# Threading a weight-streaming matmul stage through a VectorE-bound stage, matmul by matmul

## The chip, the cores and the metric

The kernel runs on one core of a Trainium2 chip. The metric is the device time of one execution in microseconds (us). The kernel before has a median of 1814.12 us over three runs (1813.09 to 1814.47). One more execution was profiled; all rows of "the profile" and "the trace" are from it. The engines are TensorE (PE; its weight loads are listed as PEld), VectorE (DVE), ScalarE (ACT), GpSimd (POOL) and SyncE (SP), which here only issues DMAs.

## The reference

One decoder layer over 512 tokens of width 1024 in float32. A convolution branch and a sliding-window attention branch are gated and added to the residual. Then comes a product-key expert layer (PEER): per token and head, two score vectors over 128 keys; the best 16 of each give the best 16 of their sums; so each token has 8 x 16 = 128 experts out of 128 x 128 = 16384, with softmax gates. Cut to what matters:

```python
def chunk(args):                                   # 128 tokens
    hx, idx, g = args                              # idx, g: 128 experts and gates per token
    a = jax.nn.gelu(jnp.einsum("ced,cd->ce", u_emb[idx], hx), approximate=False)
    return jnp.einsum("ce,ced->cd", g * a, v_emb[idx])
```

The tables u_emb and v_emb have 16384 rows of 1024 floats (4 KB each). The output is the residual plus this sum, normalised by its root mean square.

## The kernel before

**The expert layer in two ways.** Tokens 0 to 127 (`ROW_CHUNKS`) are done by gathering: for each of the 128 slots an indirect DMA on GpSimd's queue (`gathered`, L634) fetches 128 rows, one per token and 512 KB in all; VectorE multiplies and sums it (L649 for u, L657 for v). `by_rows` is a generator: each `next` emits one gather and its VectorE instruction, 256 in all, and a 257th call emits the norm and the store of these tokens (`finish`). The other 384 tokens (`DENSE`, three blocks) are done densely: for each of 128 blocks of 128 experts, a *U step* computes gelu(U x) for all 384 tokens (24 matmuls of 384 columns into a PSUM tile `mm`, then ScalarE's L674 into `ga`), and a *V step* multiplies the result with a gate matrix that is mostly zero and with V (18 matmuls of 512 columns into six PSUM tiles that accumulate over all 128 steps).

**Weights.** Float32 products are made of three products of split operands. `load_w` fetches a 512 KB block on SP's queue (`wraw`, three buffers), ScalarE rounds it (`whi`, L131), and the rest `wlo` is made either by VectorE (L137), or, while `by_dma` is set (the heads and the gate matrix), by ScalarE negating (L134) and a GpSimd DMA that adds the block again (L135). `whi` and `wlo` have four buffers each. `products` issues 16 matmuls with `whi` and then 8 with `wlo`.

**The stages that the change touches.** (1) Eight heads: `head(h)` computes scores (two blocks of 24 matmuls of 512 columns, then score matmuls L523) and the choice of experts, mostly VectorE; behind each, `U_HEADS[h]` U steps are emitted. (2) The gate matrix: for each dense token block, `keys` transposes the chosen keys, and `build_g` makes, for four tokens at a time, two comparison matrices on VectorE (`yt` L618, `xt` L621, two buffers each), multiplies them on TensorE (L626, four matmuls of 128 columns: a *gate chunk*, PSUM tile `sc`, two buffers), and ScalarE copies the result into `gst` (L628). Every 8 chunks VectorE makes `xa` and `xb` anew (L610, L612); every 4 chunks `gst` (two buffers) is stored to DRAM, 1 MB. There are 96 chunks in 24 groups. Between groups `up` emits U steps, 11 spread evenly, and three at the end (`U_LAST`). (3) The V loop: step i emits U step i + 42 (`AHEAD`) as long as there is one (86 steps), then V step i. Gate values are loaded back for eight steps at a time (`gl`, L683, two buffers), VectorE multiplies them with `ga` (L688, eight short instructions), ScalarE and VectorE split the product (`wh` L692, `wl` L693, two buffers each), and TensorE takes it (L699 to L701).

**What sets the order.** The program is written in one order, and a scheduler reorders each engine's instructions by its own estimate of when operands are ready. So the order on TensorE is not the written one: U steps whose weights are ready move ahead of gate chunks that wait for VectorE. Once built, each engine runs its list strictly in that order. The gathers in the V loop are paced by the variable `due` (L750): a U step adds twice as much as a step without one.

Of the kernel before, what the change touches and what calls it, by code (L numbers as in the profile page):

```python
# [17 lines left out]
P = 128  # L18
D = 1024
KB = D // P  # L20
S = 512
# [8 lines left out]
SLOTS = HEADS * TOPK  # L30
# [3 lines left out]
ROW_CHUNKS = (0,)  # L34
DENSE = tuple(b for b in range(NB) if b not in ROW_CHUNKS)
BUILT = DENSE
ND = len(DENSE)
NU = ND * P
CAND = 80

AHEAD = 42
U_HEADS = (4, 4, 4, 4, 3, 3, 3, 3)
U_LAST = 3
ROWS = 4
GT = 16
GI = 8
R_G = 0.0
R_V = 0.96
UC = 3
N_TAPS = 7  # L50
XT = 4
# [28 lines left out]
def body(ctx: ExitStack, tc: tile.TileContext, a, out):  # L80
    nc = tc.nc
# [9 lines left out]
    def psum(tag):  # L91
        return ps.tile([P, S], F32, name=tag, tag=tag, bufs=2)
# [19 lines left out]
    pace = [None]  # L112
# [10 lines left out]
    def fetch(src):  # L123
        raw = wp.tile([P, D], F32, name="wraw", bufs=WRAW)
        nc.sync.dma_start(raw, src)
        return raw

    def load_w(src):
        raw = fetched.pop(0) if fetched else fetch(src)
        hi = wp.tile([P, D], F32R, name="whi", bufs=WHL)  # L130
        nc.scalar.activation(hi, raw, AF.Copy)  # L131
        lo = wp.tile([P, D], F32R, name="wlo", bufs=WHL)
        if by_dma[0]:
            nc.scalar.activation(lo, hi.bitcast(F32), AF.Copy, scale=-1.0)  # L134
            nc.gpsimd.dma_start(lo, src, accum_op=OP.add)  # L135
        else:
            nc.vector.tensor_tensor(lo, raw, hi.bitcast(F32), op=OP.subtract)  # L137
        return hi, lo

    def products(p, w, x):  # L140
        wh, wl = w
        xh, xl = x
        for k in range(KB):
            ks = slice(k * P, (k + 1) * P)
            nc.tensor.matmul(p, wh[:, ks], xh[:, k], start=(k == 0), stop=False)  # L145
            nc.tensor.matmul(p, wh[:, ks], xl[:, k], start=False, stop=False)  # L146
        for k in range(KB):
            ks = slice(k * P, (k + 1) * P)
            pace[0] = nc.tensor.matmul(p, wl[:, ks], xh[:, k], start=False, stop=(k == KB - 1))  # L149

    def mm_block(src, x):
        w = load_w(src)
        p = psum("mm")
        products(p, w, x)
        return p
# [41 lines left out]
    def pair_x(name):  # L197
        return [keep.tile([P, KB, S], F32R, name=name + x, tag="x" + x) for x in "hl"]
# [225 lines left out]
    p = psum("ot")  # L424
# [12 lines left out]
    p = psum("ot")  # L437
# [11 lines left out]
    for j in range(KB):  # L449
        p = mm_block(a["w_ao"][j], oT)  # L450
        nc.vector.tensor_tensor(sga[:, j], sga[:, j], p, op=OP.mult)
    mT = pair_y("m")
    for j in range(KB):
        p = mm_block(a["w_co"][j], yT)
# [10 lines left out]
    tT = pair_x("tT")  # L465
    by_dma[0] = False
    for b0 in range(0, NB, 2):
        acc = [psum(t) for t in (("ot", "ot", "sc", "sc") if b0 == 0 else ("sc", "sc", "mm", "mm"))]
        for k in range(KB):
            hi, lo = load_w(a["w_out"][k])  # L470
            for c in range(2):
                for n in range(2):
                    ns = slice(n * 512, (n + 1) * 512)
                    p, cs = acc[2 * c + n], chunk(b0 + c)
                    nc.tensor.matmul(p, mT[0][:, k, cs], hi[:, ns], start=(k == 0), stop=False)
                    nc.tensor.matmul(p, mT[1][:, k, cs], hi[:, ns], start=False, stop=False)
            for c in range(2):
                for n in range(2):
                    ns = slice(n * 512, (n + 1) * 512)
                    nc.tensor.matmul(acc[2 * c + n], mT[0][:, k, chunk(b0 + c)], lo[:, ns], start=False,  # L480
                                     stop=(k == KB - 1))
# [115 lines left out]
    def build_g(b):  # L597
        n = BUILT.index(b)
        p = psum("tr")
        nc.tensor.transpose(p[:, :P], gate[:, b], ident)  # L600
        gT = rt.tile([P, P], F32, name="gT", bufs=2)
        nc.scalar.activation(gT, p[:, :P], AF.Copy)
        high = P // LOW
        for g in range(P // GT):
            if g * GT % XS == 0:
                xa = gp.tile([P, XS, high], F32, name="xa")
                xb = gp.tile([P, XS, LOW], F32, name="xb")
                cs = slice(g * GT, g * GT + XS)
                for t, w, k in ((xa, high, 0), (xb, LOW, 1)):
                    nc.vector.tensor_tensor(t, keyT[:, k, n, cs, None].to_broadcast([P, XS, w]),  # L610
                                            iota[:, None, :w].to_broadcast([P, XS, w]), op=OP.is_equal)
                nc.vector.tensor_tensor(xa, xa, gT[:, cs, None].to_broadcast([P, XS, high]), op=OP.mult)  # L612
            st = gp.tile([P, P, GT], F32, name="gst", bufs=2)
            for t0 in range(0, GT, XT):
                c = slice(g * GT + t0, g * GT + t0 + XT)
                cx = slice(c.start % XS, c.start % XS + XT)
                yt = gp.tile([P, XT, P], F32, name="yt", bufs=XB)
                nc.vector.tensor_tensor(yt, keyT[:, 2, n, c, None].to_broadcast([P, XT, P]),  # L618
                                        iota[:, None, :].to_broadcast([P, XT, P]), op=OP.is_equal)
                xt = gp.tile([P, XT, high, LOW], F32, name="xt", bufs=XB)  # L620
                nc.vector.tensor_tensor(xt, xa[:, cx, :, None].to_broadcast([P, XT, high, LOW]),  # L621
                                        xb[:, cx, None, :].to_broadcast([P, XT, high, LOW]), op=OP.mult)
                for t1 in range(0, XT, 4):
                    p = psum(("sc", "ot")[t1 // 4 % 2]).rearrange("p (t i) -> p t i", t=4)
                    for t in range(4):
                        nc.tensor.matmul(p[:, t], yt[:, t1 + t], xt[:, t1 + t].rearrange("p a b -> p (a b)"),  # L626
                                         start=True, stop=True)
                    nc.scalar.activation(st[:, :, t0 + t1:t0 + t1 + 4].rearrange("p i t -> p t i"), p, AF.Copy)  # L628
            nc.sync.dma_start(gv[b][:, g], st)
            yield  # L630

    def gathered(table, b, s):
        r = rows.tile([P, D], F32, name="row", bufs=ROWS)
# [32 lines left out]
    ga = {}  # L666
    gl = {}

    def u_step(i):
        w = load_w(a["put"][i])  # L670
        p = psum("mm")[:, :NU]
        products(p, w, [t[:, :, S - NU:] for t in tT])
        g = tp.tile([P, NU], F32, name="ga", bufs=AHEAD + 1)
        nc.scalar.activation(g, p, AF.Gelu)  # L674
        ga[i] = g
# [33 lines left out]
    ups = iter(range(P))  # L709

    def up(n):
        for _ in range(n):
            i = next(ups, None)
            if i is not None:
                u_step(i)

    for h in range(HEADS):
        head(h)
        up(U_HEADS[h])
    spread, groups, done = AHEAD - U_LAST - sum(U_HEADS), len(BUILT) * (P // GT), 0  # L720
    for b in BUILT:
        keys(b)
        for _ in build_g(b):
            up((done + 1) * spread // groups - done * spread // groups)
            done += 1
    up(U_LAST)
    by_dma[0] = False
    gctx.close()
    vp = ctx.enter_context(tc.tile_pool(name="vp", bufs=1, reuse_waits="tile"))
# [1 line left out]
    gf = load_g("gf")  # L731
    vacc = [psum(t) for t in ("tr", "sc", "ot") for _ in range(2)]
    rowgen = by_rows()
    total, due = 2.0 * P - AHEAD, 0.0
    load_gates(0)
    last = {}
    for i in range(P):
        up(1)
        if 0 <= i % GI - GL_AT < ND:
            load_gates(i - i % GI + GI, (i % GI - GL_AT,))  # L740
        if i < P - 2:
            v_steps(i)
        elif i == P - 2:
            for _ in rowgen:
                pass
            for n, b in enumerate(DENSE):
                last[n] = rows.tile([P, D], F32, name="row", bufs=ROWS)
                nc.sync.dma_start(last[n], x2d[b])
            v_steps(i, i + 1)
        due += (2 if i + AHEAD < P else 1) * 2 * SLOTS * len(ROW_CHUNKS) / (R_V * total)  # L750
        while due >= 1:
            due -= 1
            next(rowgen, None)
# [59 lines left out]
```

## Time and profile before

| what | value |
|---|---|
| the profiled execution's own time | 1814.3 us |
| its span, first to last instruction | 1812.5 us |
| mean granted TensorE clock | 0.980 |
| TensorE busy | 1726.6 us, 95% |
| VectorE busy | 1362.7 us, 75% |
| ScalarE busy | 907.1 us, 50% |
| GpSimd busy | 457.4 us, 25% |
| first and last gate chunk on TensorE | 702.2 and 887.8 us |
| first V matmul | 901.67 us |
| moved by DMA | 444.86 MB, mean 245 GB/s |

Busy times are sums over the whole program. The stages have different limits, so the rows to read are those of a stretch of time. A row that ends in brackets says how long the engine stood idle before it and what ended the wait.

### The profile page before, as it was taken

What the parts mean: (1) busy time and instruction counts of PE and PEld (TensorE: products, weight loads), DVE (VectorE), ACT (ScalarE), POOL (GpSimd) and SP (SyncE); (2) the same over time, 40 slices, a digit from 0 to 9 for tenths busy, and PEclk for the clock granted to TensorE, in tenths of its full rate; (3) what the DMA queues carried; (4) which work ended last, traced back from release to release, by engine and by line L of the source; (5) the groups of instructions that cost most, each with busy time, mean ns of one, the idle gap of its engine ahead of it and who ended that gap; (6) DMA issues with size and microseconds to landing.
All of it is one profiled execution on the core that took longest, in us unless ns stands there. A gap on an engine that the chain in (4) does not pass through costs nothing.

```text
span 1812.5 us, 25036 instructions
## 1 busy us (share of the span) xinstructions
PE 1726.6 (95%) x8892; PEld 1514.8 (84%) x8892; DVE 1362.7 (75%) x2755; ACT 907.1 (50%) x1287; POOL 457.4 (25%) x374
## 2 busy tenths in 40 slices
PE   7999999999999999977599999999999999999996
PEld 6887767788899999976489999999998999987775
DVE  6999992745777996688678768768768777887775
ACT  6449988645656657666433333333333333333323
POOL 1111100110111111000034335335335434434430
PEclk9999999999999999999799999999999999999998
DMA  8996554776999989743678898898888888888873
GB/s 246 225 222 148 130 116 105 166 221 213 252 215 225 212 209 245 226 178 163 232 275 294 286 353 299 288 328 315 283 319 315 306 316 316 316 310 286 289 274 105
DMA packets 165709, 444.86 MB, mean 245 GB/s; under 512 B 14544, under 2 KB 66256, under 8 KB 162512
## 3 DMA queue, kind: packets, MB, share of 16 engines
q0 software_dynamic: 53280, 194.01, 39.9%
q1 hardware_dynamic: 112304, 249.26, 38.6%
q8 instruction: 70, 1.15, 0.2%
q14 instruction: 55, 0.45, 0.1%
HBM read 410.44 MB, written 29.88 MB: 243 GB/s over the span
## 4 chain that ended last, share of the span: by engine, by line
PE 65%; issue 15%; POOL 7%; DVE 6%; DMA 5%; ACT 2%; SPq 0%; POOLq 0%; DVEq 0%; ACTq 0%
PE mm L146 14%; PE mm L145 14%; PE mm L149 14%; POOL row L634 7%; PE sc L626 4%; DMA row<-pv,eidx 2%; PE tr L700 2%; PE tr L701 2%; PE tr L699 2%; PE sc L699 2%; PE sc L700 2%; DMA gl<-gb 2%; PE ot L699 2%; PE sc L701 2%; PE ot L700 2%
## 5 line engine op out<-in xcount | busy, mean ns | idle before, releaser
L131 ACT ACTIVATE whi<-wraw 128x1024 fp32r<-128x1024 f32 x346 | 365.3, 1057 | 447.1 <-DMA wraw<-put 172.3
L145 PE MATMUL mm<-tTh,whi 128*128 128x384 f32 (+2 forms) x1168 | 395.3, 340 | 1.5 <-ACT wlo L134 1.4
L146 PE MATMUL mm<-tTl,whi 128*128 128x384 f32 (+2 forms) x1168 | 396.5, 340 | 0.2 <-DVE tTl L192 0.2
L137 DVE TENSOR_TENSOR wlo<-wraw,whi 128x1024 fp32r<-128x1024 f32 x232 | 283.1, 1223 | 51.0 <-ACT whi L131 50.1
L634 POOL DMA_INDIRECT row<-pu,eidx x128 | 176.2, 1377 | 402.7 <-DVE row L649 254.4
L634 POOL DMA_INDIRECT row<-pv,eidx x128 | 182.2, 1424 | 255.1 <-DVE acc L657 241.2
L149 PE MATMUL mm<-tTh,wlo 128*128 128x384 f32 (+2 forms) x1168 | 234.8, 339 | 0.0
L145 PEld LDWEIGHTS mm<-tTh,whi 128*128 128x128 f32 x1168 | 219.6, 188 | 10.0 <-ACT wlo L134 1.8
L146 PEld LDWEIGHTS mm<-tTl,whi 128*128 128x128 f32 x1168 | 219.5, 188 | 8.3 <-DVE tTl L192 0.4
L149 PEld LDWEIGHTS mm<-tTh,wlo 128*128 128x128 f32 x1168 | 204.0, 188 | 3.8
L692 ACT ACTIVATE wh<-gl 128x384 fp32r<-128x384 f32 x128 | 67.1, 524 | 274.2 <-PE ot L700 255.3
L657 DVE SCALAR_TENSOR_TENSOR acc<-row,gate,acc 128x1024 f32<-128x1024 f32 x128 | 164.1, 1282 | 13.7 <-DMA row<-pv,eidx 7.3
L649 DVE SCALAR_TENSOR_TENSOR row<-row,hrow 128x1024 f32<-128x1024 f32 x128 | 155.3, 1223 | 21.7 <-DMA row<-pu,eidx 20.8
L294 DVE SCALAR_TENSOR_TENSOR yconv<-uc,pc,yconv 128x512 f32<-128x512 f32 x240 | 169.0, 748 | 0.4
L688 DVE TENSOR_TENSOR gl<-gl,ga 128x384 f32<-128x384 f32 x128 | 61.8, 554 | 104.4 <-DMA gl<-gb 104.4
L145 PE MATMUL mm<-hTh,whi 128*128 128x512 f32 (+1 forms) x352 | 135.9, 389 | 1.0 <-ACT hTh L191 0.8
L146 PE MATMUL mm<-hTl,whi 128*128 128x512 f32 (+1 forms) x352 | 135.2, 387 | 1.6 <-DVE hTl L192 1.6
L626 PE MATMUL sc<-xt,yt 128*128 128x128 f32 x768 | 110.5, 298 | 27.1 <-DVE xt L621 25.7
L626 PEld LDWEIGHTS sc<-xt,yt 128*128 128x128 f32 x768 | 101.2, 208 | 36.0 <-ACT gst L628 20.6
L628 ACT ACTIVATE gst<-sc 128x512 f32<-128x512 f32 x96 | 99.1, 1068 | 59.5 <-PE sc L626 57.6
L134 ACT ACTIVATE wlo<-whi 128x1024 fp32r<-128x1024 f32 x114 | 120.2, 1054 | 9.7 <-PE mm L149 9.0
L699 PE MATMUL tr<-whi,wh 128*128 128x512 f32 x256 | 101.3, 398 | 16.5 <-ACT wh L692 13.6
(252 smaller groups left out, 3080.5 us busy)
## 6 DMA issues: line engine op xcount, KB each, us to landing
wraw<-put SPq DMA_DIRECT2D x128, 512.0 KB, 6.3
wraw<-pv SPq DMA_DIRECT2D x128, 512.0 KB, 5.9
gb<-gst SPq DMA_DIRECT2D x24, 1024.0 KB, 3.8
gl<-gb SPq DMA_DIRECT2D x48, 512.0 KB, 9.2
wraw<-w_in SPq DMA_DIRECT2D x42, 512.0 KB, 5.3
wlo<-put POOLq DMA_DIRECT2D x42, 512.0 KB, 7.3
wlo<-w_in POOLq DMA_DIRECT2D x40, 512.0 KB, 6.5
wraw<-w_out SPq DMA_DIRECT2D x16, 512.0 KB, 3.4
```

What stands on the lines that cost most here:

```text
L131: nc.scalar.activation(hi, raw, AF.Copy)
L134: nc.scalar.activation(lo, hi.bitcast(F32), AF.Copy, scale=-1.0)
L137: nc.vector.tensor_tensor(lo, raw, hi.bitcast(F32), op=OP.subtract)
L145: nc.tensor.matmul(p, wh[:, ks], xh[:, k], start=(k == 0), stop=False)
L146: nc.tensor.matmul(p, wh[:, ks], xl[:, k], start=False, stop=False)
L149: pace[0] = nc.tensor.matmul(p, wl[:, ks], xh[:, k], start=False, stop=(k == KB - 1))
L294: nc.vector.scalar_tensor_tensor(y[:, j], uc[:, t:t + S], w, y[:, j], op0=OP.mult, op1=OP.add)
L626: nc.tensor.matmul(p[:, t], yt[:, t1 + t], xt[:, t1 + t].rearrange("p a b -> p (a b)"), start=True, stop=True)
L634: ins = nc.gpsimd.indirect_dma_start(out=r, out_offset=None, in_=table, in_offset=bass.IndirectOffsetOnAxis(ap=eidx[:, ROW_CHUNKS.index(b) ...
L649: nc.vector.scalar_tensor_tensor(r, r, 1.0, h, op0=OP.mult, op1=OP.mult, accum_out=dots[:, s:s + 1])
L657: nc.vector.scalar_tensor_tensor(acc, r, gate[:, b, s:s + 1], acc, op0=OP.mult, op1=OP.add)
L699: nc.tensor.matmul(p, w[0][:, chunk(n)], v[0][:, ns], start=(i == 0), stop=False)
```

## The change

The heads get 25 U steps instead of 28, and nothing is spread by groups any more. The remaining 17 of the first 42 become a generator, `u_threaded`, that yields after every matmul. `build_g` now yields after every gate chunk instead of every group, and at each yield the main loop draws three or four U matmuls (3.6 on the mean). Each of them is pinned with `keep_in_program_order`: the scheduler must leave it behind the instruction that was written before it on TensorE. What is left of the 17 blocks is drawn behind the last chunk. The weights of the next block are loaded when a block begins. In the V loop, a step with a U block now emits 1.48 + 1.03 = 2.51 gathers and one without 1.03, in place of 2.49 and 1.25. The number of matmuls, loads and gathers is the same.

```diff
-U_HEADS = (4, 4, 4, 4, 3, 3, 3, 3)
-U_LAST = 3
+U_HEADS = (4, 3, 3, 3, 3, 3, 3, 3)
+U_PIECE = 3.6
...
-R_V = 0.96
+ROWS_U, ROWS_V = 1.48, 1.03
...
-    def products(p, w, x):
+    def each_product(p, w, x):
         wh, wl = w
         xh, xl = x
...
+        terms = [(wh, k, t[:, k]) for k in range(KB) for t in (xh, xl)]
+        terms += [(wl, k, xh[:, k]) for k in range(KB)]
+        for n, (v, k, t) in enumerate(terms):
+            pace[0] = nc.tensor.matmul(p, v[:, k * P:(k + 1) * P], t, start=(n == 0), stop=(n == len(terms) - 1))
+            yield pace[0]
+
+    def products(p, w, x):
+        for _ in each_product(p, w, x):
+            pass
...
                     nc.scalar.activation(st[:, :, t0 + t1:t0 + t1 + 4].rearrange("p i t -> p t i"), p, AF.Copy)
+                    yield
             nc.sync.dma_start(gv[b][:, g], st)
-            yield
...
+    def u_threaded(n):
+        w = load_w(a["put"][next(ups)])
+        for i in range(sum(U_HEADS), sum(U_HEADS) + n):
+            following = load_w(a["put"][next(ups)]) if i < sum(U_HEADS) + n - 1 else None
+            for m in u_pieces(i, w):
+                tc.keep_in_program_order(m)
+                yield
+            w = following
...
-    spread, groups, done = AHEAD - U_LAST - sum(U_HEADS), len(BUILT) * (P // GT), 0
+    pieces = u_threaded(AHEAD - sum(U_HEADS))
+    share = 0.0
     for b in BUILT:
         keys(b)
         for _ in build_g(b):
-            up((done + 1) * spread // groups - done * spread // groups)
-            done += 1
-    up(U_LAST)
+            share += U_PIECE
+            while share >= 1:
+                share -= 1
+                next(pieces, None)
+    for _ in pieces:
+        pass
...
-        due += (2 if i + AHEAD < P else 1) * 2 * SLOTS * len(ROW_CHUNKS) / (R_V * total)
+        due += ((ROWS_U if i + AHEAD < P else 0.0) + ROWS_V) * len(ROW_CHUNKS)
```

**TensorE while the gate matrix is built.** In the rows below `mm` is a U block's matmul, `sc<-xt,yt` a gate chunk's, and `tr<-whi,wh` the first V step's. Before, two chunks (x8) stand behind each U block until the U blocks that were emitted run out; then come 280 chunk matmuls, 70 chunks, in one piece, and the V loop directly behind them:

```order
L626 MATMUL sc<-xt,yt 128x128 x8
L145 MATMUL mm<-tTh,whi 128x384
L146 MATMUL mm<-tTl,whi 128x384
L145 MATMUL mm<-tTh,whi 128x384
L146 MATMUL mm<-tTl,whi 128x384
L145 MATMUL mm<-tTh,whi 128x384
L146 MATMUL mm<-tTl,whi 128x384
L145 MATMUL mm<-tTh,whi 128x384
L146 MATMUL mm<-tTl,whi 128x384
L149 MATMUL mm<-tTh,wlo 128x384 x8
L626 MATMUL sc<-xt,yt 128x128 x280
L699 MATMUL tr<-whi,wh 128x512
```

With the change, every chunk (x4) has three or four U matmuls behind it, from the first chunk to the last:

```order
L628 MATMUL sc<-xt,yt 128x128 x4
L146 MATMUL mm<-tTh,whi 128x384
L146 MATMUL mm<-tTl,whi 128x384
L146 MATMUL mm<-tTh,whi 128x384
L628 MATMUL sc<-xt,yt 128x128 x4
L146 MATMUL mm<-tTl,whi 128x384
L146 MATMUL mm<-tTh,whi 128x384
L146 MATMUL mm<-tTl,whi 128x384
L146 MATMUL mm<-tTh,whi 128x384
L628 MATMUL sc<-xt,yt 128x128 x4
```

Between the last score matmul of the heads and the first chunk TensorE has 169 U matmuls before and 49 with the change; between the last chunk and the first V matmul it has none before and 100 with the change.

**VectorE in the V steps without a U block.** `gl<-gl,ga` is the multiply of the gate values of the next eight steps, `wl` the operand of one step, `acc<-row,gate,acc` one gathered row. Before, at one of the three places:

```order
L657 SCALAR_TENSOR_TENSOR acc<-row,gate,acc 128x1024
L137 TENSOR_TENSOR wlo<-wraw,whi 128x1024
L693 TENSOR_TENSOR wl<-gl,wh 128x384
L688 TENSOR_TENSOR gl<-gl,ga 128x24x16 x6
L137 TENSOR_TENSOR wlo<-wraw,whi 128x1024
L688 TENSOR_TENSOR gl<-gl,ga 128x24x16 x2
L657 SCALAR_TENSOR_TENSOR acc<-row,gate,acc 128x1024
L693 TENSOR_TENSOR wl<-gl,wh 128x384
```

With the change, at the same place:

```order
L659 SCALAR_TENSOR_TENSOR acc<-row,gate,acc 128x1024
L695 TENSOR_TENSOR wl<-gl,wh 128x384
L137 TENSOR_TENSOR wlo<-wraw,whi 128x1024
L690 TENSOR_TENSOR gl<-gl,ga 128x24x16 x8
L695 TENSOR_TENSOR wl<-gl,wh 128x384
```

Before, the multiply stands behind the 98th step's wl, with the change behind the 97th's; and all eight now stand ahead of the next wl. At the boundary before this one and at the one behind it, it also moves up by one wl; at the last one its place is the same, but eight multiplies instead of five stand ahead of the next wl.

**SP's queue at the end.** `wraw<-pv` are V blocks for the last steps, `row<-x2d` the residuals that the last additions need; these go into the buffers of the last gathered rows and wait for them. Before:

```order
L683 DMA gl<-gb_82 128x8x128
L125 DMA wraw<-pv 128x1024 x5
L748 DMA row<-x2d_76 128x1024
L748 DMA row<-x2d_77 128x1024
L748 DMA row<-x2d_78 128x1024
L125 DMA wraw<-pv 128x1024 x2
L664 DMA out<-wraw 128x1024
L125 DMA wraw<-pv 128x1024 x5
```

With the change:

```order
L685 DMA gl<-gb_82 128x8x128
L125 DMA wraw<-pv 128x1024 x10
L764 DMA row<-x2d_76 128x1024
L764 DMA row<-x2d_77 128x1024
L764 DMA row<-x2d_78 128x1024
L125 DMA wraw<-pv 128x1024 x2
L666 DMA out<-wraw 128x1024 x4
```

The residuals' loads, and the norm of the gathered tokens, moved from seven V blocks ahead of the end to two.

More of the change, by code (lines that the diff above doesn't have):

```diff
@@ L138, in load_w @@
         return hi, lo
-    def products(p, w, x):
+    def each_product(p, w, x):
         wh, wl = w
         xh, xl = x
[L143 to L149, printed above, removed]
+        terms = [(wh, k, t[:, k]) for k in range(KB) for t in (xh, xl)]
[6 more added lines that the diff above has]
+            pass
     def mm_block(src, x):
@@ L667, in body, with u_pieces @@
     gl = {}
-    def u_step(i):
-        w = load_w(a["put"][i])
+    def u_pieces(i, w):
         p = psum("mm")[:, :NU]
-        products(p, w, [t[:, :, S - NU:] for t in tT])
+        for m in each_product(p, w, [t[:, :, S - NU:] for t in tT]):
+            yield m
         g = tp.tile([P, NU], F32, name="ga", bufs=AHEAD + 1)
@@ L714, in up @@
             if i is not None:
-                u_step(i)
+                for _ in u_pieces(i, load_w(a["put"][i])):
+                    pass
[7 more added lines that the diff above has]
+            w = following
     for h in range(HEADS):
@@ L723, in body @@
         for _ in build_g(b):
-            up((done + 1) * spread // groups - done * spread // groups)
-            done += 1
-    up(U_LAST)
+            share += U_PIECE
[3 more added lines that the diff above has]
+    for _ in pieces:
+        pass
     by_dma[0] = False
@@ L733, in body @@
     rowgen = by_rows()
-    total, due = 2.0 * P - AHEAD, 0.0
+    due = 0.0
     load_gates(0)
```

## The prediction

> **What bounds the kernel now.** I read the stretches table first (time from the start, then its length; busy us with instruction counts of TensorE, its weight loads, VectorE, ScalarE, GpSimd; granted clock; DMA share; GB/s).
>
> ```profile
> 650.00:700.00 50.00, 50.00 (x284) 48.01 (x283) 44.90 (x213) 34.46 (x43) 9.11 (x11) 1.00 0.93 219
> 700.00:750.00 50.00, 50.00 (x343) 49.96 (x342) 25.86 (x42) 33.71 (x40) 6.62 (x8) 1.00 0.93 262
> 750.00:800.00 50.00, 43.03 (x295) 41.10 (x295) 39.13 (x62) 30.28 (x34) 0.00 (x0) 0.98 0.48 183
> 800.00:850.00 50.00, 38.59 (x248) 34.64 (x247) 44.05 (x74) 33.62 (x32) 0.00 (x0) 0.88 0.36 149
> 850.00:900.00 50.00, 29.35 (x192) 26.12 (x192) 31.53 (x53) 25.11 (x24) 3.42 (x3) 0.84 0.60 224
> ```
>
> TensorE is full through the heads (to about 700) and, by the page's slices, through the V loop (from 910 on); it is the bound there. Between them, while the gate matrix is built, two halves do not meet: from 700 to 750 TensorE is full and VectorE half idle (25.86 of 50); from the next stretch on VectorE is busy (44.05 of 50) and TensorE idles, and its clock falls too (0.88, 0.84). Who waits for whom between 700 and 960 (waiting engine and tile, releaser: us, times, longest):
>
> ```profile
> DVE yt L618 <- PE sc L626: 40.0, 28, 3.4
> PE sc L626 <- DVE xt L621: 25.7, 35, 2.2
> PE tr L699 <- ACT wh L692: 13.6, 1, 13.6
> ```
>
> First VectorE waits for TensorE, then TensorE for VectorE, and at the end TensorE stands 13.6 us until the first V step. The change goes at all three.
>
> **The prices.** A U block is 24 matmuls; a gate chunk is four matmuls of two records each. TensorE in the full part, in time (start, us, line, tile):
>
> ```profile
> 753.93 1.95 PE L626 MATMUL sc<-xt,yt 128*128 128x128 f32 x16
> 755.63 0.42 PE L146 MATMUL mm<-tTl,whi 128*128 128x384 f32 x1
> 755.89 0.34 PE L145 MATMUL mm<-tTh,whi 128*128 128x384 f32 x1
> 759.70 1.95 PE L626 MATMUL sc<-xt,yt 128*128 128x128 f32 x16
> ```
>
> Two chunks take 755.63 - 753.93 = 1.70, so 0.85 each. From 755.89 to 759.70 run 22 U matmuls: 0.173 each. The first one behind a chunk takes 0.26: 0.09 for the switch. VectorE and TensorE in the idle part:
>
> ```profile
> 783.02 0.42 DVE L610 TENSOR_TENSOR xa<-keyT,iota 128x256 f32<-128x256 f32 x1
> 784.29 0.69 DVE L618 TENSOR_TENSOR yt<-keyT,iota 128x512 f32<-128x512 f32 x1
> 786.90 0.69 DVE L618 TENSOR_TENSOR yt<-keyT,iota 128x512 f32<-128x512 f32 x1 [0.71 <-PE sc L626]
> 787.50 0.69 DVE L621 TENSOR_TENSOR xt<-xa,xb 128x512 f32<-128x512 f32 x1
> 886.93 1.13 PE L626 MATMUL sc<-xt,yt 128*128 128x128 f32 x8 [0.27 <-DVE xt L621]
> ```
>
> One operand costs VectorE 0.60 start to start (787.50 - 786.90), so a chunk's two cost 1.2 (1.29 to the last result). Every eighth chunk has 784.29 - 783.02 = 1.27 on top. A chunk gives its result 1.13 after it starts.
>
> **Part 1, the heads.** Three U blocks leave heads 1 to 3. TensorE is full there, so 72 x 0.173 = 12.5 us go, if VectorE keeps up; at 650:700, where the heads already have three blocks, it works 44.90 of 50 while TensorE is full, so it does. The last head's last score matmul and VectorE's keys behind it:
>
> ```profile
> L523 PE MATMUL sc<-sk,pq x32: 270/275/275, 640.5 to 671.9; 128*128 128x128 f32 x32
> 690.83 0.29 DVE L591 SCALAR_TENSOR_TENSOR k_q<-k_p,sel 128x128 f32<-128x128 f32 x1
> 694.51 0.23 DVE L590 CAST k_p<-k_u 128x128 f32<-128x128 uint32 x1 [2.83 <-PE tr L594]
> 698.04 1.29 DVE L621 TENSOR_TENSOR xt<-xa,xb 128x512 f32<-128x512 f32 x2
> ```
>
> The score matmul (671.9) moves to 659.4 and the keys (691.1) to 678.6. TensorE has 49 U matmuls left before the first chunk (169 before), 8.5 us, and then nothing: it is dry from 668 until the keys come. This is a new wait of the change. From the keys, 0.4 for the transposes, 698.04 + 0.69 - 694.51 = 4.2 for the first operands, and about 1.0 (estimated from the short key rows) because the third chunk of tokens' keys now stand ahead of the first gate chunk on TensorE: it starts at 678.6 + 5.6 = 684.2, after 16 us without work.
>
> **Part 2, the threaded loop.** 96 chunks, each with 3.6 U matmuls behind it: 0.85 + 0.09 + 3.6 x 0.173 = 1.56 of TensorE; VectorE needs 1.2 + 1.27/8 = 1.37, so TensorE is the bound. With two buffers, the operands of the next chunk but one start when a chunk's result is there: 1.13 + 1.29 = 2.42 after its start, while TensorE wants them after 3.13. The slack is 0.7. At each boundary of eight chunks VectorE puts 1.27 in, and mostly another yt of 0.60 ahead of the xt that is awaited: 1.27 + 0.60 - 0.7 is about 1.1 late, 11 times, 12 us. ScalarE has one eviction per chunk and, per 24 U matmuls, three more instructions, two gaps apart: they fit in the slack of 0.9; one activation table load falls between two evictions, 1.3. The weights are split about 26 chunks ahead of their use, so the queues of SP and GpSimd that bring them have some 40 us. What the clock does behind the 16 us pause, the trace shows at the V loop's start:
>
> ```profile
> 888.10 1.02 ACT L628 ACTIVATE gst<-sc 128x512 f32<-128x512 f32 x1 [0.36 <-PE sc L626]
> 900.50 3.84 DVE L688 TENSOR_TENSOR gl<-gl,ga 128x384 f32<-128x384 f32 x8 [13.72 <-DMA gl<-gb]
> 901.67 0.80 PE L699 MATMUL tr<-whi,wh 128*128 128x512 f32 x1 [13.61 <-ACT wh L692]
> 902.69 0.63 PE L699 MATMUL tr<-whi,wh 128*128 128x512 f32 x1
> 903.12 0.63 PE L700 MATMUL tr<-wlo,wh 128*128 128x512 f32 x1
> ```
>
> After 13.6 us of idling a matmul takes 0.43 (903.12 - 902.69) where it takes 0.226 in a V step that is warm, for the first twelve: 2.4 us. I take 3 for the loop's cold start. It ends at 684.2 + 96 x 1.56 + 12 + 1.3 + 3 = 850.
>
> The same pause has a page of its own: the Trainium skill (TensorE: Matmul & The Clock Gate, HAM oscillation) says that pauses over about 3.4 us bring the half clock back, which this row bears out (0.43 against 0.226 behind 13.6 us). By it the pause at 668 costs, as an estimate, 3.4 us at half rate, so 1.7 us; the sum goes by the 3 from the row.
>
> **Part 3, the hand-over.** From the last chunk's result (888.06) to the first V matmul (901.67) run eviction, store, load, multiply: 13.6 us, with TensorE idle. Now 100 U matmuls, 17.3 us, stand there: the idling is covered with 3.7 to spare (without cover it costs 13.6), and the V loop starts warm at 867. Before, 1080 U matmuls were done by then, now 1042, so 38 x 0.173 = 6.6 are owed: 874 against 901.7 + 2.4 = 904. **Gain: 30 us.**
>
> **Part 4, the gathers' pace.** In U steps 2.51 rows instead of 2.49: TensorE is full, nothing. In the 42 steps without U, 1.03 rows instead of 1.25, at 1.28 of VectorE each. VectorE is not the bound there: a step is 18 x 0.2265 = 4.08 of TensorE, and VectorE's is 1.2 + 0.56 + 0.55 + 1.25 x 1.28 = 3.9. What stops TensorE is this:
>
> ```profile
> DVE gl L688 <- DMA gl<-gb: 21.4, 3, 7.5
> PE tr L701 <- DVE wl L693: 10.5, 3, 3.8
> 1640.38 0.56 DVE L693 TENSOR_TENSOR wl<-gl,wh 128x384 fp32r<-128x384 f32 x1
> 1648.54 0.56 DVE L693 TENSOR_TENSOR wl<-gl,wh 128x384 fp32r<-128x384 f32 x1 [1.19 <-ACT wh L692]
> 1655.92 2.90 DVE L688 TENSOR_TENSOR gl<-gl,ga 128x384 f32<-128x384 f32 x6 [6.82 <-DMA gl<-gb]
> 1662.00 0.55 DVE L693 TENSOR_TENSOR wl<-gl,wh 128x384 fp32r<-128x384 f32 x1
> 1640.97 5.46 SPq L683 DMA_DIRECT2D gl<-gb  x3
> 1660.00:1670.00 10.00, 7.39 (x20) 5.87 (x21) 10.00 (x12) 1.75 (x3) 6.33 (x3) 0.66 0.69 236
> ```
>
> The gate values of the next eight steps can be fetched only when the last wl of the eight before the current ones has been made (1640.38, fetched at 1640.97), they land 15 us later, and VectorE stands before the multiply with everything behind it, the next wl too. Three times TensorE stops for 3.5 (10.5 in all), and the clock dips behind it (0.66: of 7.39 busy 2.5 are lost here; I take 1.6 for each, since this is the deepest). The change moves the multiply one step, 4.08, up on VectorE at two of the three places (and at one where nothing waited): In the rows TensorE wanted the wl 3.7 before it was there (1662.55), 18.5 behind 1640.38; a step earlier that is 14.4. With the same landing (15.5 behind) and eight multiplies of 0.48 it would wait 15.5 + 8 x 0.48 + 0.55 - 14.4 = 5.5. Against that, 0.22 rows of 512 KB less in 4.08 us are some 27 GB/s less, and the fetch lands sooner. Between 1 (landing after 11) and 5.5 I take 3.5, as now: nothing gained.
>
> At the end, the last two weight fetches now stand on SP's queue behind the loads that wait for the last rows, and on ScalarE behind the row result's norm:
>
> ```profile
> 1765.66 1.06 ACT L180 ACTIVATE wraw<-acc 128x1024 f32<-128x1024 f32 x1 [1.82 <-DVE acc L657]
> 1767.99 1.28 ACT L170 ACT_TABLE_LOAD   x1
> 1776.64 1.06 ACT L131 ACTIVATE whi<-wraw 128x1024 fp32r<-128x1024 f32 x1 [5.25 <-DMA wraw<-pv]
> 1760.00:1770.00 10.00, 7.58 (x34) 5.95 (x32) 3.23 (x8) 4.19 (x7) 0.00 (x0) 1.00 0.51 193
> 1770.00:1780.00 10.00, 9.51 (x34) 7.24 (x35) 6.21 (x9) 4.07 (x6) 0.00 (x0) 0.83 0.64 212
> ```
>
> Step 126 starts after wh 0.53, square 1.06 + 0.18, table 1.28, root 0.20, whi 1.06: TensorE idles 4.3, and 2.6 for the clock (as above). The same place costs 2.42 + 0.49 of idling and 9.51 x 0.17 = 1.6 of clock now, 4.5, so 2.4 more. **Part 4: 2 to 3 us lost.**
>
> **Sum.** The profiled execution took 1814.3 (0.2 above the median of 1814.12): 1814.3 - 30 + 3 = **1787**.
>
> **Rivals.**
> - The last stage is relieved: the fetch lands before VectorE comes to it, the three stops of 3.5 + 1.6 go: 15 us more, **1772**. For it: fewer rows on a full DMA; against: the multiply stands earlier.
> - The loop beats slower than its parts: from 800 to 850 TensorE did 248/8 = 31 chunks, 1.6 each, without any U matmul, so the engines' hand-overs count. At 1.75 for 1.56: 18 us, **1805**. Against: slack of 0.7 and 0.9 that the idle part had not.
> - Slower: the clock stays down through the loop. With small gaps the grant fell before:
>
> ```profile
> 820.00:830.00 10.00, 7.70 (x48) 7.23 (x48) 8.40 (x15) 6.03 (x6) 0.00 (x0) 0.83 0.41 173
> ```
>
> At a grant g the chunk takes 1.56/g; the gain of 27 is gone at 1.56/g = 1.84, g = 0.85. At 0.75 it is 96 x 0.52 = 50 longer: **1837**. Against: there TensorE was 7.7 busy of 10; here a chunk leaves gaps only at the boundaries, 1.1 in 13.6. The Trainium skill (TensorE: Matmul & The Clock Gate, A second HAM failure mode: psum-queue depth-cycling) speaks for this rival: small idle times between groups of matmuls that go round PSUM banks, as the chunks do here, make the clock swing. The 0.83 above agrees with it; the loop of the change no run has shown yet.
>
> That the change does nothing can be left out: TensorE's order is pinned.
>
> **Chances.** Forecast 0.57, last stage relieved 0.16, slow loop 0.16, clock 0.11. A difference under 0.2% (3.6 us) cannot be told from none. Of the slow loop 0.15 and of the clock 0.02 stay faster, 0.01 and 0.03 are the same, the clock's other 0.06 slower: faster 0.90, same 0.04, slower 0.06. The range goes from just below the relieved stage, 1769, to the slow loop, 1804; beyond lie some 0.1 for the clock and 0.07 below.
>
> **What would show it.** The loop's step in a stretches table, 13.6 per eight chunks, with TensorE over 9 of 10 at a clock of 1; a pause of about 16 before the first chunk and none before the first V step; the first V matmul near 867; three waits of VectorE for gl; a stop of 4 before the last two steps. A loop over 1.7 a chunk, or a clock under 0.9 in it, would make the prediction wrong.

## The result, and the profile after

The changed kernel takes 1781.83 us (median of 4, 1780.71 to 1783.15) against 1814.15; the ratio is 0.9823, 95% interval 0.9806 to 0.9840. Forecast was 1787 in a range of 1769 to 1804: 5 us too much. Its profiled execution took 1780.9, with a span of 1779.1 from the first to the last instruction (1812.5 before); the rows below are from it.

The stretches of the changed kernel, in the columns of the table in the prediction:

```profile
650.00:700.00 50.00, 36.72 (x221) 33.94 (x220) 44.09 (x164) 26.93 (x33) 4.65 (x6) 0.86 0.57 141
700.00:750.00 50.00, 46.66 (x351) 45.47 (x350) 42.43 (x69) 39.66 (x45) 4.01 (x5) 1.00 0.80 244
750.00:800.00 50.00, 45.66 (x342) 44.50 (x342) 42.76 (x71) 39.87 (x44) 3.47 (x4) 1.00 0.82 261
800.00:850.00 50.00, 46.72 (x345) 45.60 (x344) 39.69 (x65) 39.20 (x43) 7.99 (x8) 1.00 0.87 275
850.00:900.00 50.00, 48.84 (x253) 44.88 (x253) 36.56 (x56) 17.44 (x24) 15.45 (x10) 1.00 0.85 298
```

The two halves now meet: from 700 to 850 TensorE is busy 46 of 50 at a clock of 1.00 and VectorE 40 to 43. Before, TensorE had 50.00, 43.03 and 38.59 of 50 there, and the stage went on to 888, with 29.35 of 50 from 850 to 900 and a clock of 0.84. The new hole is in the first row: 36.72. TensorE's instructions at the four places that the forecast named (start, us, line, tile, in brackets the idle time before it and what ended it):

```profile
667.09 1.55 PE L146 MATMUL mm<-tTh,wlo 128*128 128x384 f32 x8
678.79 0.48 PE L596 MATMUL tr<-ident,k_p 128*128 128x128 f32 x1 [10.15 <-DVE k_p L592]
684.05 2.07 PE L628 MATMUL sc<-xt,yt 128*128 128x128 f32 x8
686.88 1.05 PE L628 MATMUL sc<-xt,yt 128*128 128x128 f32 x8
753.33 1.13 PE L628 MATMUL sc<-xt,yt 128*128 128x128 f32 x8 [1.06 <-DVE xt L623]
766.83 1.13 PE L628 MATMUL sc<-xt,yt 128*128 128x128 f32 x8 [1.24 <-ACT gst L630]
864.67 0.50 PE L701 MATMUL tr<-whi,wh 128*128 128x512 f32 x1 [1.16 <-ACT wh L694]
```

The U matmuls run out at 668.6, the keys' transposes come at 678.8, the first gate chunk at 684.05. The two boundaries of eight chunks shown are 753.33 to 766.83, 13.5 apart, and each stops TensorE for a little over 1 us, once for VectorE and once for ScalarE. At the end of the build TensorE stands idle for 1.16 alone: the first V matmul is at 864.67, where it was at 901.67.

The waits from 690 to 850 (waiting engine and tile, releaser: us, times, longest), and then the last U matmuls, which end at 1569.3, and the stops of TensorE in the steps without U behind them:

```profile
PE sc L628 <- DVE xt L623: 9.3, 9, 1.2
PE sc L628 <- ACT gst L630: 2.9, 3, 1.2
```

```profile
1567.73 1.55 PE L146 MATMUL mm<-tTh,wlo 128*128 128x384 f32 x8
1593.17 1.22 PE L703 MATMUL tr<-whi,wl 128*128 128x512 f32 x2 [4.81 <-DVE wl L695]
1629.84 0.73 PE L703 MATMUL tr<-whi,wl 128*128 128x512 f32 x2 [1.39 <-DVE wl L695]
1664.73 0.73 PE L703 MATMUL tr<-whi,wl 128*128 128x512 f32 x2 [1.96 <-DVE wl L695]
1700.39 1.04 PE L703 MATMUL tr<-whi,wl 128*128 128x512 f32 x2 [2.70 <-DVE wl L695]
1756.46 1.22 PE L701 MATMUL tr<-whi,wh 128*128 128x512 f32 x2 [3.88 <-ACT whi L131]
```

So the account, with all steps taken from the two profiled executions, is: 37.0 gained when V starts; 704.6 us from there to the last U matmul against 701.6, because more U is owed, so 34.0 when the steps without U start; these take 198.3 against 197.9, and the end 11.6 against 11.3. That is 33.4 of span (within rounding), and all of it was gained before 865.

### The profile page after: what moved, and what is told of

Its sections match the earlier page's. It is cut to its first block, busy times and chain, and to the rows that moved or that the text cites. A ratio compares the mean times of both kernels' runs of the same rounds, so it can differ in the third digit from the quotient of the medians.

```text
span 1779.1 us, 25055 instructions
## 1 busy us (share of the span) xinstructions
PE 1708.0 (96%) x8892; PEld 1501.4 (84%) x8892; DVE 1366.0 (77%) x2755; ACT 905.6 (51%) x1287; POOL 458.6 (26%) x374
## 5 line engine op out<-in xcount | busy, mean ns | idle before, releaser
L146 PE MATMUL mm<-tTh,wlo 128*128 128x384 f32 (+2 forms) x1168 | 240.5, 341 | 0.0
L695 DVE TENSOR_TENSOR wl<-gl,wh 128x384 fp32r<-128x384 f32 x128 | 70.9, 554 | 76.6 <-ACT wh L694 76.6
L628 PE MATMUL sc<-xt,yt 128*128 128x128 f32 x768 | 103.2, 278 | 12.2 <-DVE xt L623 9.3
L628 PEld LDWEIGHTS sc<-xt,yt 128*128 128x128 f32 x768 | 99.1, 193 | 16.3 <-ACT gst L630 10.2
```

Of the source, the lines that this page charges most:

```text
L146: pace[0] = nc.tensor.matmul(p, v[:, k * P:(k + 1) * P], t, start=(n == 0), stop=(n == len(terms) - 1))
L695: nc.vector.tensor_tensor(wl3, w, wh3.bitcast(F32), op=OP.subtract)
```

## The experiments

All are changes of the changed kernel, but for the last. Its 1781.8 is the number to compare with. The medians of the kernel before, measured anew beside each group of runs, lie between 1812.0 and 1814.2, so a difference under the 3.6 of the prediction is not told from nothing here either. Times inside a run are from its one profiled execution.

**1. The hand-over without its cover** (third part of the forecast). All threaded matmuls go into the loop and the next two U blocks are held behind the first V step.

```
-U_PIECE = 3.6
+U_PIECE = 4.25
...
-        up(1)
+        up(0 if i == 0 else 2 if i == 1 else 1)
```

(The three U blocks and the first two V steps of that place are also held in the program's order.)

> The changed kernel with all its threaded U matmuls inside the loop (4.25 for 3.6 behind each chunk), none behind the last chunk, and the next two U blocks held behind the first V step: nothing covers the way from the last chunk to the first V step. Theory (the third part of the forecast: without cover it costs 13.6): the loop is 66 x 0.173 = 11.4 longer less some 2 of its stops, TensorE then stands 13.6, the V loop begins cold (2.4), and 34 U matmuls (5.9) are owed less the 5.9 that no longer stand ahead of V: 12 to 16 slower, 1794 to 1798. Rival: the hand-over has become short because operands and store no longer queue up, or is hidden by other work anyway: 1780 to 1786.

1798.69 (1796.70 to 1801.22): 16.9 slower, just beyond the 12 to 16 expected. TensorE around the hand-over in this run:

```profile
856.45 1.12 PE L146 MATMUL mm<-tTh,wlo 128*128 128x384 f32 x5
871.45 0.79 PE L701 MATMUL tr<-whi,wh 128*128 128x512 f32 x1 [13.88 <-ACT wh L694]
874.65 0.80 PE L705 MATMUL tr<-whi,wl 128*128 128x512 f32 x1 [1.98 <-DVE wl L695]
877.37 0.60 PE L705 MATMUL sc<-whi,wl 128*128 128x512 f32 x1
879.88 0.33 PE L146 MATMUL mm<-tTh,whi 128*128 128x384 f32 x1
```

The 13.6 of before are back as 13.88, so the hand-over had not become shorter: the U matmuls cover it. The first V step takes 879.88 - 871.45 = 8.4 where a warm one (at full clock) takes 4.08; that cold start is 4.3, more than the 2.4 that was taken from before, because the second wait of 1.98 falls into it. The expectation had counted 2.4. First V 6.8 later, 34 U matmuls (5.9) still owed, 4.3 of cold start: 17.0, the measured 16.9.

**2. Three blocks back into the heads, and 3. four blocks into the pause.** Both move U blocks out of the loop.

```
-U_HEADS = (4, 3, 3, 3, 3, 3, 3, 3)
-U_PIECE = 3.6
+U_HEADS = (4, 4, 4, 4, 3, 3, 3, 3)   # run 2, with U_PIECE = 2.8
+U_HEADS = (4, 3, 3, 3, 3, 3, 3, 7)   # run 3, with U_PIECE = 2.6
```

> The changed kernel with the three U blocks put back into heads 1 to 3, and 2.8 for 3.6 U matmuls behind each gate chunk, so that as many as before stand behind the last one. Theory (only TensorE's idle time counts, and work moved between two full stretches is worth nothing): the first chunk is 12.5 later, the loop 96 x 0.8 x 0.173 = 13.3 shorter, but the slack of two chunks falls from 0.7 to about 0.43, so each of 11 boundaries stops TensorE 0.3 longer: 1781 to 1786. Rival: taking blocks out of the heads is itself a gain of 12.5: then 1794. Rival: with 2.8 the loop falls to the pace it had alone (1.6 a chunk): the loop does not shorten and the time is 1794 too, but the loop's step tells which.

> The changed kernel with four of the threaded U blocks moved in front of the first gate chunk, where TensorE has nothing for 16 us, and 2.6 for 3.6 U matmuls behind each chunk. Theory: the first chunk stays at 684, the loop has 96 x 0.173 = 16.6 less to do; its chunk is 1.39 of TensorE against VectorE's 1.37, the slack falls to 0.36, so a boundary costs 1.5 for 1.1, 4.6 in all: 12 gained, 1770 (1767 to 1775). Rival: the loop has no slack left and beats at the 1.6 that chunks alone took: no gain, 1780 to 1784. Rival: the moved blocks' ScalarE and queue work holds up the keys, the first chunk comes several us later, and half of the gain is lost, 1776.

Run 2: 1791.77 (1790.94 to 1794.41), 10 slower. Run 3: 1780.41 (1779.98 to 1781.04), no gain. Both expectations of the theory failed, and at the same place: run 2's loop gave back 4.2 of 13.3, from 161.8 to 157.6 (first to last chunk's matmul: 698.0 to 855.6), run 3's 6.6 of 16.6 (692.4 to 847.6). "Work moved between two full stretches is worth nothing" does not hold, for the loop is not full: with less U in it, its stops grow. Run 3's 155.2 is 1.62 a chunk, the beat of its first rival. The waits from 690 to 860 in run 3:

```profile
PEld sc L628 <- ACT gst L630: 20.2, 20, 1.9
PE sc L628 <- DVE xt L623: 12.0, 9, 1.6
PE sc L628 <- ACT gst L630: 3.3, 9, 1.6
```

Against 9.3 and 2.9 in the changed kernel, TensorE now waits 12.0 and 3.3, and its weight loads 20.2 for ScalarE's evictions, where they waited 10.2. In run 3 the pause itself was filled, but one block or two too far, which is its second rival. The same view from 640 to 700:

```profile
DVE k_p L592 <- PE tr L596: 5.8, 1, 5.8
```

The transposes of the keys stand behind 145 U matmuls on TensorE, VectorE waits for them, and the first chunk comes at 692.4.

**4. Half of that into the pause.**

```
+U_HEADS = (4, 3, 3, 3, 3, 3, 3, 5)   # with U_PIECE = 3.1
```

> The changed kernel with two of the threaded U blocks moved in front of the first gate chunk (four made the transposes of the keys wait behind them on TensorE, 5.8 us), and 3.1 for 3.6 behind each chunk. Theory now: the pause is filled to 677, before the keys come at 678.6, so the first chunk stays at 684 to 685; the loop, read between the runs with 2.8 (1.64 a chunk) and 3.6 (1.685), takes 159 for 161.8: 2 to 3 gained, 1779. Rival, the plain count of TensorE's idle time: 8.3 gained, 1773.5. Rival: the keys come later again: 1782 or more.

1778.67 (1774.59 to 1781.14), as the corrected theory had it: first chunk at 683.6, loop 159.4. Of 8.3 us of filled pause 2.4 are left by the loop; the difference in time is too small to be told from none.

**5. Three operand buffers, 6. four PSUM banks**: what holds the loop?

```
-XB = 2
-AHEAD = 42
-U_PIECE = 3.6
+XB = 3          # run 5
+AHEAD = 40
+U_PIECE = 3.1
...
-                    p = psum(("sc", "ot")[t1 // 4 % 2])
+                    p = psum(("sc", "ot")[(g * GT + t0) // XT % 2])   # run 6, alone
```

> The changed kernel with three buffers for the gate chunks' operands in place of two. The memory for them comes from running U two blocks less ahead (40 for 42) and so 3.1 for 3.6 U matmuls behind each chunk, with as many as before left behind the last. Two blocks less in the loop and two more in the V loop are 8.3 us each way if nothing else moves. Theory (the stops at each eight chunks come from VectorE having only two buffers of lead): of the loop's 12.2 us of stops the 9.3 for VectorE's xt go, the loop is 96 x 1.476 + 3 = 145 for 161.8, and 8.3 are owed later: 1773. Rival (what holds the loop with fewer U matmuls is something else, as in the two runs with 2.8 and 2.6, whose loops took 158 and 156): 159, and the 8.3 owed: 1787.

> The changed kernel with the gate chunks going round four PSUM banks in place of two, nothing else. Theory (ScalarE, whose evictions stand behind the weights' splits and the Gelus of the U blocks, is a second limit of the loop that the forecast did not have): of the loop's 12.2 us of TensorE stops the 2.9 for the eviction go, and the weight loads that waited 10.2 for it come in time: 3 to 5 gained, 1777 to 1779. Rival: the stops that count are VectorE's alone (9.3), and an eviction that is not waited for is only late at the next place: 1781 to 1783.

Run 5: 1777.88 (1775.38 to 1780.28), some 4 faster, between its theory (1773) and its rival (1787). Run 6: 1782.01 (1779.74 to 1784.05), nothing, as its rival had it. Run 5's waits in the loop (690 to 848):

```profile
PE sc L628 <- ACT gst L630: 8.0, 6, 2.1
PEld sc L628 <- ACT gst L630: 12.6, 15, 2.4
```

No wait for xt is left: the stops at the boundaries did come from two buffers of lead. But 8.0 for ScalarE's evictions came in their place, so the loop takes 152.2, between the 145 of the theory and the 159 of the rival, and the 8.3 that are owed eat most of it up. Four banks without the third buffer change nothing (162.2); TensorE still waited 8.4 there for xt and 3.5 for evictions.

**7. The gate multiplies held in order.** What stops TensorE in the steps without U is VectorE in front of a load, not the load being too late for its step; the forecast said so, and left the stops where they were.

```
-        nc.vector.tensor_tensor(w, w, ga[i].rearrange("p (g t) -> p g t", t=GT), op=OP.mult)
+        m = nc.vector.tensor_tensor(w, w, ga[i].rearrange("p (g t) -> p g t", t=GT), op=OP.mult)
+        tc.keep_in_program_order(m)
```

> The changed kernel with the multiply of the gate values (VectorE, one for each step) held in the program's order, so that it stands just ahead of its own step instead of eight at once ahead of a load that has not landed. Theory: TensorE's stops in the steps without U (10.9 us in four, and the clock behind them, some 1.5 to 2.5 each) come from VectorE standing in front of the first multiply with the next step's operands queued behind: they go, 12 to 16 us gained, 1766 to 1770. Rival: the load is late for its own step too: the stops stay, 1780 to 1784. Rival: the single multiplies break up VectorE's row work and each costs a hand-over: 1775 or more with many short stops.

1764.91 (1761.87 to 1765.27): 16.9 gained, just beyond the 12 to 16 expected. VectorE at such a place, first in the changed kernel, then in this run:

```profile
1653.21 1.23 DVE L137 TENSOR_TENSOR wlo<-wraw,whi 128x1024 fp32r<-128x1024 f32 x1 [0.39 <-ACT whi L131]
1660.37 3.84 DVE L690 TENSOR_TENSOR gl<-gl,ga 128x384 f32<-128x384 f32 x8 [5.93 <-DMA gl<-gb]
1664.12 0.55 DVE L695 TENSOR_TENSOR wl<-gl,wh 128x384 fp32r<-128x384 f32 x1
```

```profile
1657.71 0.55 DVE L690 TENSOR_TENSOR gl<-gl,ga 128x384 f32<-128x384 f32 x1
1658.18 1.28 DVE L659 SCALAR_TENSOR_TENSOR acc<-row,gate,acc 128x1024 f32<-128x1024 f32 x1
1659.38 0.55 DVE L696 TENSOR_TENSOR wl<-gl,wh 128x384 fp32r<-128x384 f32 x1
```

Eight multiplies stood in a row before a load for which VectorE waited 5.93, with the next step's wl behind them. One at a time, none waits for the load in the whole stage (four waits, 27.6 us, in the changed kernel). The steps without U, in the changed kernel and in this run:

```profile
1570.00:1600.00 30.00, 25.19 (x101) 20.27 (x101) 19.19 (x25) 7.66 (x11) 8.71 (x7) 0.89 0.68 224
1690.00:1720.00 30.00, 27.30 (x113) 22.09 (x113) 22.11 (x27) 9.44 (x13) 9.08 (x7) 0.94 0.76 271
```

```profile
1570.00:1600.00 30.00, 30.00 (x135) 24.94 (x134) 24.37 (x28) 10.70 (x16) 12.66 (x9) 1.00 0.86 291
1690.00:1720.00 30.00, 30.00 (x134) 24.86 (x133) 28.50 (x34) 11.33 (x16) 16.50 (x9) 1.00 0.78 270
```

They take 181.7 us where they took 198.3.

**8. The old pace of the rows** (fourth part of the forecast).

```
-        due += ((ROWS_U if i + AHEAD < P else 0.0) + ROWS_V) * len(ROW_CHUNKS)
+        due += (2 if i + AHEAD < P else 1) * 2 * SLOTS * len(ROW_CHUNKS) / (0.96 * total)
```

> The changed kernel with the old pace of the row gathers (2.49 rows in a U step, 1.25 in a step without U). The forecast's fourth part says that the new pace costs 2 to 3 us: 1779 to 1780. The trace of the change says less: its steps without U take 198.3 us against 197.9, so the pace is worth nothing and the time stays at 1782 within 2. Rival: the new pace had relieved the last stage and something else took it back; then the old pace is slower by 5 or more, 1787 or above.

1780.23 (1778.99 to 1780.80): 1.6 less, not to be told from none. Its last stop is 2.9 against 3.88. The new pace relieved nothing, and the forecast's cost of 2 to 3 for it is at best 1.6 of the whole time. In the steps without U alone it looks larger: 195.7 us with the old pace against 198.3, while the way from the first V matmul to the last U matmul is 1.1 longer (705.7 for 704.6).

**9. The pin** (the held multiplies of run 7) **with 1.10 rows** in a step without U, so that the rows end four steps earlier.

```
-ROWS_U, ROWS_V = 1.48, 1.03
+ROWS_U, ROWS_V = 1.42, 1.10
```

> The run with the gate multiplies held in order, with 1.10 rows for 1.03 in a step without U, so that the last rows are done some four steps before the end. Theory: the last stop of TensorE (4.3 and 0.7 us, and the clock behind it) comes from the row result's norm and the loads for it standing ahead of the last two steps' weights: it goes, 4 to 7 gained on that run's 1765: 1758 to 1761. Rival: VectorE then lacks the time for the rows in those steps, and short stops take its place: 1763 to 1768.

1763.55 (1761.84 to 1764.94): 1.4 less than run 7, not to be told from none, and not the 4 to 7 expected. The time is the rival's, though short stops by VectorE came to no more than the 0.72 below. TensorE's stop moved with the norm of the row result, from 4.3 at the end to this:

```profile
1729.54 0.50 PE L702 MATMUL tr<-whi,wh 128*128 128x512 f32 x1 [2.24 <-ACT wh L695]
```

and 0.72 at one other place. In both runs a step's wh stands behind the norm on ScalarE.

**10 and 11. Together.** The pin, 1.42 and 1.10 rows, three buffers with U 40 ahead, two U blocks into the pause, 2.56 U matmuls behind each chunk; run 11 with four banks too.

> Multiplies held in order, 1.10 rows, three operand buffers with U 40 ahead, two U blocks in front of the first chunk, 2.56 U matmuls behind each. If the buffers were the loop's limit, the loop takes 96 x 1.39 + 3 = 136 to 140 for 161.8, 8.3 owed: 1743 to 1748. If the loop is held by something else at 1.6 a chunk, 154 and 8.3 owed: 1758 to 1762, no better than the run with rows alone.

> The run of all together (1754.6) with four PSUM banks. There TensorE waited 8.5 us for evictions and 1.6 for operands in the loop, which took 148.4 where its TensorE work is 96 x 1.39 = 133. Theory: the eviction's stops go: 1745 to 1749. Rival: the evictions themselves wait for the store of the tile before last to land (9.0 us in five places there): the stops move there and 1752 to 1756 is left.

Run 10: 1754.56 (1754.37 to 1756.63), between its two cases. Run 11: 1750.99 (1748.91 to 1752.74; ratio to the kernel before 0.9652, 0.9637 to 0.9667), 30.8 below the changed kernel, and between its own theory (1745 to 1749) and rival (1752 to 1756). Against run 10 it is 3.57 less, which is just too little to be told from none. The waits in run 11's loop:

```profile
PE sc L628 <- DVE xt L623: 2.8, 10, 0.4
PE sc L628 <- ACT gst L630: 0.3, 1, 0.3
ACT gst L630 <- DMA gb<-gst: 15.7, 9, 3.8
```

With four banks TensorE hardly feels the evictions, though ScalarE itself waits 15.7 for the stores: the rival's stop is there and is hidden. The loop is 12.2 shorter than run 10's, but most of that goes elsewhere. Its first chunk comes at 687.3, 3.4 later than in run 10; the heads' last score matmul was already 3.3 later, in a part that the edit does not touch. And TensorE then stands in front of the first V matmul, for 4.42 where it was 0.49 in run 10:

```profile
844.29 0.50 PE L702 MATMUL tr<-whi,wh 128*128 128x512 f32 x1 [4.42 <-ACT wh L695]
```

The hand-over is no longer covered. The loops side by side, with TensorE's work as 96 x (0.94 + n x 0.173), by the prices of the prediction (some 4.5 too much in each row, as the next section shows):

| run | U per chunk | operand buffers, banks | first to last matmul, us | TensorE's work |
|---|---|---|---|---|
| changed kernel | 3.6 | 2, 2 | 161.8 | 150 |
| run 6 | 3.6 | 2, 4 | 162.2 | 150 |
| run 4 | 3.1 | 2, 2 | 159.4 | 142 |
| run 2 | 2.8 | 2, 2 | 157.6 | 137 |
| run 3 | 2.6 | 2, 2 | 155.2 | 133 |
| run 5 | 3.1 | 3, 2 | 152.2 | 142 |
| run 10 | 2.56 | 3, 2 | 148.4 | 133 |
| run 11 | 2.56 | 3, 4 | 136.2 | 133 |

With two buffers, one U matmul less per chunk is 16.6 of work and 6.6 of time. The third buffer takes away one limit and shows the next; the banks help only behind it.

**12. The pin on the kernel before.** The edit of run 7 on the kernel before.

> The kernel before, with its gate multiplies held in the program's order, nothing of the change. Theory (the three stops of the last stage are the kernel's own, and the change leaves them): the 10.5 us of waiting and some 4.8 of clock go here too, so 1797 to 1801, much the same gain as the 17 on the changed kernel. Rival: with the old pace of rows, 1.25 for 1.03 in a step without U, VectorE has too little time between the single multiplies, and short stops take their place: 1804 or more.

1802.93 (1800.25 to 1806.86): 10.3 gained, less than expected and not the rival either. The steps without U take 187.2 for 197.9, against 181.7 for 198.3 on the changed kernel. What is left of stops there:

```profile
1695.49 0.73 PE L702 MATMUL tr<-whi,wl 128*128 128x512 f32 x2 [1.33 <-DVE wl L694]
1729.93 0.72 PE L702 MATMUL tr<-whi,wl 128*128 128x512 f32 x2 [1.32 <-DVE wl L694]
1758.23 0.79 PE L700 MATMUL tr<-whi,wh 128*128 128x512 f32 x1 [4.87 <-ACT wh L693]
```

So the stops for the gate values are the old kernel's own. That the pin brings 6 more on the changed kernel may be the new pace's doing, which would then be worth nothing with the eight multiplies in a row and some us without them. The changed kernel with the pin and the old pace was not run, so this stays open.

## Why the prediction was right, point by point

- **Heads, and the new pause: right.** 12.5 off the heads put the last score matmul at 659.9 (forecast 659.4), the keys at 678.8 (678.6) and the first chunk at 684.05 (684.2). Run 2, with the blocks back in the heads, starts its first chunk 14 later.
- **Cold start of the loop: mis-sized, 3 for 1.4.** First to second chunk took 686.88 - 684.05 = 2.83, where 0.85 + 0.09 + 3 x 0.173 = 1.46 is warm. The row that was taken for it, the cold start of V behind 13.6 us, is one of 128x512 matmuls with nothing ahead of them; here twelve transposes had run first, in two groups behind idle times of 10.15 and 1.86. That this makes the difference is likely and not shown by a run. The 1.7 that the prediction worked out, as an estimate, from the Trainium skill (TensorE: Matmul & The Clock Gate, What's actually happening) was nearer.
- **The threaded loop: near in size, with errors that partly cancel.** The first chunk's start to the last chunk's end took 161.9; the forecast was 96 x 1.56 + 12 + 1.3 + 3 = 166, last chunk at 846 for 850. Beside the cold start, the price of a chunk was too high. Two chunks that ran without a stop, with three U matmuls between:

```profile
688.48 1.05 PE L628 MATMUL sc<-xt,yt 128*128 128x128 f32 x8
689.89 1.05 PE L628 MATMUL sc<-xt,yt 128*128 128x128 f32 x8
```

  That is 1.41 where the prices give 1.46; with four it is 1.59 for 1.63, and these are the medians of the whole loop. Over 96 chunks that is some 4.5 less, so TensorE's work was 145 and not 150. Waiting was larger than counted: less the 1.4 of cold start some 15 of the 161.9 are left for it, against 12 and 1.3. The waits listed above hold 12.2 of it, 9.3 for VectorE and 2.9 for ScalarE, whose evictions the sum held to fit in their slack; the rest are waits too short for the list. That the loop is bound by TensorE was true at 3.6 U matmuls to about 0.9 of its time, and no longer at 2.6 to 2.8: runs 2 and 3, expected by the same reasoning, missed their ranges by 6 and 5 us.
- **The slow-loop rival did not come true at 3.6 U matmuls,** but what it says shows with fewer: run 3's chunk takes 1.62 where its parts say 1.39.
- **The clock rival fell.** 1.00 in every stretch from 700 to 900, with stops of 1.06 and 1.24 at the boundaries. The rule that spoke for this rival (the Trainium skill, TensorE: Matmul & The Clock Gate, A second HAM failure mode: psum-queue depth-cycling) did not come true in this loop, which goes round two PSUM banks and leaves some 7% of TensorE idle.
- **The hand-over: right that it is covered,** and shown by run 1: 13.88 come back when the cover goes. V starts at 864.67 (867). But the 3.7 to spare were not there. From the last eviction (846.21) to the first V matmul it took 18.5, not 13.6, so that TensorE still stood 1.16. The last store and the load that waits for it, on SP's queue:

```profile
847.30 0.32 SPq L632 DMA_DIRECT2D gb<-gst  x1
855.70 7.42 SPq L685 DMA_DIRECT2D gl<-gb  x6
```

  From the one to the other are 8.4, where it was 889.15 to 893.08 before, 3.9. Between 847 and 856 DMA moved 368 GB/s, against 264 from 889 to 893 before, so the store has other transfers beside it, such as a weight block issued at 850.64; that they delay it is likely, and no run parts it.
- **What is owed: 4.2 forecast (6.6 of U less 2.4 of cold start), 3.0 measured.** A wait of TensorE for wlo, 0.7 in the V loop of before, is gone and is part of the difference. Gain at the last U matmul 34.0 for 30.
- **Steps without U: 2 to 3 lost was forecast, 0.4 measured, and that is in part luck.** The stops for the gate values stayed (10.9 in four for 10.5 in three), so "last stage relieved" fell. The end came nearly as forecast: the final stop grew from 2.9 to 3.88 (forecast 4.3), and the 24 matmuls behind it took 8.2 for 7.4 before, where warm ones take 5.4. So 1.0 of stop and 0.8 of clock were lost there, for 2.4 forecast. What made up for it are the stops for the gate values: two of the four (1.39 and 1.96) had no slow matmul behind them, so that the clock cost 4.5 behind the four, against 6.5 behind the three before. Nothing in the prediction says why. Over the stage, less the 774 V matmuls at 0.2265, 23.0 of stops and clock are left against 22.6 before.
- **Two slips in the working, too small to matter.** The 2.6 for the clock in the last steps is 2.5 by the row that it points back at. The 3.6 U matmuls behind the last chunk (0.6 us) are counted in the loop and once more among the 100 behind it.

Against the profiled 1780.9 the forecast is 6 too high: 2.3 at the start of V (the last chunk came some 4 early, and the hand-over took part of that back), 1.2 in what is owed, some 2 in the last stage.

## What to carry to other kernels

When two engines take turns at being idle, threading the one's spare work between the other's pieces is worth the idle time that it removes, and it can be counted ahead row by row to some us. But a loop so threaded has several limits, one behind the other, and the sum for one mix of work does not hold for another: here 0.6 to 0.7 of a matmul's time came back as stops when it was taken out (runs 2 to 4). And an instruction that a scheduler has hoisted in front of a load that is late holds up all that stands behind it on its engine; holding it at its own step brought 17 us for two lines here, and 10 on the kernel before.

## What the runs showed of the hardware that was not expected

The stop behind which the clock falls is not of one length. A pair of V matmuls at full speed takes 0.62 within a step and 0.73 as the first behind a stop, and 24 of them take 5.4. In the changed kernel's rows above, the 24 behind the stops of 1.39 and 1.96 us took 5.6; behind 2.70 they took 7.2, behind 4.81 they took 7.9. Two rows of run 6, one of run 5 and one of run 8:

```profile
1591.70 1.07 PE L703 MATMUL tr<-whi,wl 128*128 128x512 f32 x2 [2.33 <-DVE wl L695]
1628.92 0.80 PE L703 MATMUL tr<-whi,wl 128*128 128x512 f32 x2 [2.68 <-DVE wl L695]
```

```profile
1666.65 0.73 PE L703 MATMUL tr<-whi,wl 128*128 128x512 f32 x2 [2.65 <-DVE wl L695]
```

```profile
1702.37 0.73 PE L703 MATMUL tr<-whi,wl 128*128 128x512 f32 x2 [3.07 <-DVE wl L695]
```

Behind the first two the 24 took 7.2, behind the others 5.6 and 5.7. So a stop of 2.33 cost speed and one of 3.07 did not, and the 3.4 us that the prediction named is no firm bound here. What else decides there, no run shows. The first pair alone does not tell: in the kernel before it took 0.73 behind a stop of 3.78, and the slow matmuls came after it.
